# The first chunk's attention beside the third phase of the projection; scores in front of transposes; output weights by halves

## The chip, the cores and the metric

The kernel runs on one core of a Trainium2 chip. Such a core has several engines that each work through a queue of their own in order: TensorE (PE, matrix products and transposes; its weight loads are listed as PEld), VectorE (DVE), ScalarE (ACT), GpSimd (POOL) and SyncE (SP, here a queue that issues transfers). An instruction waits for the semaphores of those that it depends on, and all that stands behind it on its engine waits with it. The metric is the device time in microseconds (us) from launch to end; several runs are given, and the profile comes from one execution that was recorded in full.

## The reference

One layer of a hybrid decoder, for one prompt of 4096 tokens and for 64 sample tokens, 4160 rows in all. Three groups of heads are fed by one projection, gated, joined to a width of 1024 and projected once more:

```python
def _layer(x, conv_buf, buf_k, buf_v, mem_k, mem_v, g_pre, g_post, w_in, conv_w, sink, w_out, prompt):
    h = _rmsnorm(x, g_pre)
    z = h @ w_in
    cb, cc, ch, cg, q, k, v, ag, mq, mg = _split_cols(z)
    ...
    out_a = jax.nn.silu(cg) * cb * conv
    ...
    o_b = _window_prompt(q, k, v, sink_g)
    ...
    out_b = jax.nn.silu(ag) * o_b
    o_c = _mem_attend(mq.reshape(n, t, MEM_HEADS, HEAD_DIM), mem_k, mem_v)
    out_c = jax.nn.silu(mg) * o_c
    y = jnp.concatenate([out_a, out_b, out_c], axis=-1) @ w_out
    return x + _rmsnorm(y, g_post), new_conv, new_k, new_v
```

Group A is a gated convolution of width 3. Group B is attention with 8 query heads and 2 key heads of 64 in a window of 128 keys, with a learned sink logit per head, worked out in blocks of 128 queries against their own and the previous 128 keys. Group C is attention with 4 heads over 256 memory tokens. All is in float32.

## The kernel before

**Projection.** `input_projection` (from L841) computes z transposed, columns on the partitions, in three phases (`PHASES`, L43). A phase takes some pairs of column blocks of 128, and goes through eight blocks of 520 rows; a block is computed from seven products of halves (`PRODUCTS`, L40, a Strassen scheme over halves of 260 rows). So the steps are (phase, block, product); the third phase has 3 pairs ("quads"), 8 x 7 = 56 steps, and in each step `product` (L340) issues 36 matmuls of 128x260 over high and low parts of operands in fp32r, and `evict` (L348) adds the result from PSUM to the block's z on DVE, or copies it on ACT. `h_load` fetches the operand of three steps later into a rotating pool (`hx`, 6 buffers) and `split` (L332) makes the high part on ACT (L335) and the low part on DVE (L336). The first phase leaves the gates in DRAM (`md`) and keys and values (`qd`, `vd`), the second makes the convolution, the third the queries; a finished block is split into high and low parts (L386, L388) and stored to `qd` from SP. A step's further tasks are spread among its quads as "jobs". In the third phase the first jobs (`third_jobs`) make the memory's keys and values, then (13 steps behind the second block's start) load keys and queries of chunk 0. In the last block of this phase the output weights are loaded and split into high and low parts (`wo_load`, `wo_split`), row block by row block, left and right half of the columns in turn.

**Attention.** Prompt rows are taken in 16 chunks of 256 (`Chunk`, L978). A chunk loads keys `kst` (L998) and queries `q` (L1009) on POOL's queue, values `vT` and the gates `mix` on SP's. `values` transposes the values (L1022). A chunk has two window pairs and two cross pairs, and a pair two units. A window unit computes scores `ws` (L1093), copies and masks them into `sm` (L1095 ACT, L1096 DVE), takes the maximum (L1098), four exponentials (L1106), and divides (reciprocal, a factor of 0.5 at L1111, product at L1112); then it transposes them (`wt`, L1116), copies them out (L1118) and masks by POOL's selects (L1123 into `wpv`, L1126 in place). A cross unit has scores `xs` (L1053), maximum (L1054), exponentials (L1057), reciprocal (L1058), POOL's scale (L1061), transposes `xt` (L1066). When both units of a pair are done, `both_values` (L969, products at L976) multiplies by the values and DVE multiplies the gate in `mix` by the result (L1041, L1080).

`Pipe` staggers the units. One `start()` does, in this order: the value products of a pair whose second unit was begun three starts ago, the transposes of the unit begun two starts ago, and the scores of a new unit.

**Output projection.** `Block` (L1298) is for 128 rows: `load` the rows of x, `split` the mix into `mh` and `ml` (L1321 ACT, L1322 DVE), then `run`: for each of two halves of 512 columns, 8 row blocks of 3 matmuls `y` (L1339) with a `start()` ahead of row blocks 2 and 6; the half is multiplied by `gpost` (L1346) and squared and summed (L1347), and at the end normalised and added to x (L1357).

**Order.** Behind the projection `open_attention` closes the projection's pools (PSUM then has 3 banks for y, 2 for scores, 2 for transposes, 1 for value products). Chunks 0 and 1 follow, 16 starts with nothing between. Then `gpost` is loaded and scaled (L1296), and chunk c (from 2 on) runs beside blocks 2c-4 and 2c-3, four starts to a block. 29 blocks carry starts; the sample's attention and the last blocks follow. Outside the first phase, whose order is that of the text, a scheduler places each engine's instructions by its own estimates and due times; the engines run their queues in that order.

## Time and profile before

| | before |
|---|---|
| three runs, us | 1622.83, 1626.41, 1627.67 (median 1626.41) |
| the profiled execution, us | 1625.52 |
| its span, first to last instruction, us | 1623.8 |
| mean granted clock of TensorE | 0.992 |
| DMA packets, bytes | 175108, 305.63 MB |
| stores of q, k parts `qd` from SP | 2 x 48 issues |

The third phase lies at about 690 to 940 us, chunks 0 and 1 alone from 940 on, blocks beside chunks from 979.6 to about 1540, the sample and the last blocks to the end.

How to read the profile: busy times are shares of one execution's span. In a table of stretches each row is a window of time; the counts in brackets are instructions. A timeline row gives the start, the length, the engine, the line, the operation with output and inputs, and in square brackets the idle time before it with the instruction that ended it. Matmuls are pipelined: a modelled length of 0.39 us for a 128x512 matmul stands beside a distance of 0.23 us between starts. A float32 product (not fp32r) appears as two records.

### The profile page before, as it was taken

How to read it: one execution, taken by the hardware profiler on the slowest of the kernel's cores; microseconds unless marked ns; L12 is line 12 of the kernel's file. 1: busy time of each engine (PE TensorE's matmuls, PEld its weight loads, DVE VectorE, ACT ScalarE, POOL GpSimd, SP SyncE). 2: the span in 40 equal slices, each digit the busy share in tenths (PEclk: the TensorE clock that was granted, in tenths of full speed). 3: DMA queues.
4: the chain of work that ended last, by engine and by line, in shares of the span. 5: the costliest groups of instructions: out<-in, count | busy, mean ns of one | idle time of the engine just before them, and what ended most of it. 6: DMA issues, size and time to landing. Idle time of an engine off the chain costs nothing.

```text
span 1623.8 us, 29613 instructions
## 1 busy us (share of the span) xinstructions
PE 1579.5 (97%) x11099; PEld 1395.2 (86%) x11099; DVE 1182.6 (73%) x2131; ACT 790.8 (49%) x2023; POOL 345.8 (21%) x590
## 2 busy tenths in 40 slices
PE   9999999999999999999999979999999999999998
PEld 9999999999999999988999955777777777777766
DVE  6778888899988777964766777667776777676733
ACT  6766665565222222443443456555555555555522
POOL 0222222210000000010000035444333443443210
PEclk9999999999999999999999989999999999999999
DMA  9978999776544334699666699766666676665152
GB/s 272 206 209 225 272 284 264 270 231 231 195 171 153 119 119 147 226 291 268 205 235 251 225 281 142 139 140 140 140 153 144 151 152 144 140 140 117 53 192 91
DMA packets 175108, 305.63 MB, mean 188 GB/s; under 512 B 31093, under 2 KB 104565, under 8 KB 174933
## 3 DMA queue, kind: packets, MB, share of 16 engines
q1 hardware_dynamic: 128069, 226.76, 44.6%
q0 software_dynamic: 46176, 75.92, 24.4%
q8 instruction: 88, 1.44, 0.4%
q10 hardware_dynamic: 720, 1.05, 0.2%
q14 instruction: 55, 0.45, 0.1%
HBM read 196.54 MB, written 108.12 MB: 188 GB/s over the span
## 4 chain that ended last, share of the span: by engine, by line
PE 65%; DVE 17%; ACT 6%; issue 5%; DMA 4%; POOL 3%; SPq 0%; ACTq 0%; POOLq 0%; DVEq 0%
PE c L345 45%; PE y L1339 10%; ACT sm L1106 4%; DVE sm L1112 2%; PE wo L976 2%; PE wt L1116 2%; DVE sm L1096 2%; PE ws L1093 2%; DVE wmx L1098 1%; PE xs L1053 1%; POOL xp L1061 1%; PE xo L976 1%; PE xt L1066 1%; DVE xr L1357 1%; DVE ml L1322 1%
## 5 line engine op out<-in xcount | busy, mean ns | idle before, releaser
L1339 PE MATMUL y<-wo,mh 128*128 128x512 f32 (+1 forms) x1072 | 351.0, 391 | 2.3 <-DVE mh L1316 1.4
L352 DVE TENSOR_TENSOR z<-c,z 128x520 f32<-128x520 f32 (+1 forms) x308 | 194.3, 645 | 88.2 <-PE c L345 87.0
L1339 PEld LDWEIGHTS y<-wo,mh 128*128 128x128 f32 x1072 | 200.3, 188 | 44.2 <-issue 4.0
L1339 PE MATMUL y<-wo,ml 128*128 128x512 f32 (+1 forms) x520 | 202.7, 390 | 1.2 <-DVE ml L1322 1.2
L1106 ACT ACTIVATE sm<-sm,wnm 128x128 f32<-128x128 f32 x256 | 99.9, 391 | 76.4 <-DVE wnm L1100 76.4
L1339 PEld LDWEIGHTS y<-wo,ml 128*128 128x128 f32 x520 | 98.2, 189 | 16.4 <-DVE ml L1322 1.6
L998 POOL DMA_DIRECT2D kst<-qd x64 | 38.9, 622 | 251.3 <-DVE sm L1112 183.7
L1123 POOL TENSOR_SCALAR_AFFINE_SELECT wpv<-wpt 128x512 f32<-128x512 f32 x62 | 39.6, 638 | 222.8 <-ACT wpt L1118 222.0
L1093 PE MATMUL ws<-kst,q 128*128 128x256 f32 x512 | 79.6, 295 | 0.6 <-ACT sm L1095 0.6
L1054 DVE TENSOR_REDUCE xmx<-xs 128x2 f32<-128x512 f32 x64 | 44.1, 690 | 42.5 <-PE xs L1053 42.4
L1057 ACT ACTIVATE xp<-xs,xnm 128x256 f32<-128x256 f32 x128 | 59.3, 468 | 31.6 <-DVE xnm L1055 25.2
L1095 ACT COPY sm<-ws 128x256 f32<-128x256 f32 x128 | 44.3, 371 | 59.7 <-PE ws L1093 56.6
L711 POOL CAST wmask<-negs 128x256 uint8<-128x256 f32 x1 | 1.3, 1259 | 321.0 <-DMA negs<-in_wmask 321.0
L1061 POOL TENSOR_SCALAR xp<-xp,xrd 128x256 f32<-128x256 f32 x128 | 61.7, 488 | 36.8 <-DVE xrd L1058 34.1
L1347 ACT ACTIVATE y<-y 128x512 f32<-128x512 f32 (+1 forms) x66 | 38.8, 588 | 62.1 <-DVE yn L1346 62.0
L1093 PEld LDWEIGHTS ws<-kst,q 128*128 128x128 f32 x512 | 66.3, 191 | 2.4 <-ACT sm L1095 1.0
L1346 DVE TENSOR_TENSOR yn<-y,gpost 128x512 f32<-128x512 f32 (+1 forms) x66 | 45.0, 682 | 30.2 <-PE y L1339 29.8
L1357 DVE SCALAR_TENSOR_TENSOR xr<-yn,yst,xr 128x1024 f32<-128x1024 f32 (+2 forms) x34 | 42.5, 1252 | 28.0 <-POOL yst L1353 28.0
L1116 PEld LDWEIGHTS wt<-ident,sm 128*128 128x128 f32 x256 | 27.7, 143 | 37.7 <-ACT xp L1057 19.4
L1066 PEld LDWEIGHTS xt<-ident,xp 128*128 128x128 f32 x256 | 29.1, 141 | 33.0 <-PE wo L976 10.5
L1116 PE MATMUL wt<-ident,sm 128*128 128x128 f32 x256 | 41.8, 287 | 15.2 <-DVE xrd L1058 8.4
L1118 ACT COPY wpt<-wt 128x512 f32<-128x512 f32 x64 | 36.9, 577 | 39.2 <-PE wt L1116 38.5
(959 smaller groups left out, 5133.3 us busy)
## 6 DMA issues: line engine op xcount, KB each, us to landing
q<-qd POOLq DMA_DIRECT2D x64, 384.0 KB, 6.1
mix<-md SPq DMA_DIRECT2D x16, 1024.0 KB
xr<-in_x_p SPq DMA_DIRECT2D x32, 512.0 KB
nat<-in_x_p SPq DMA_DIRECT2D x39, 416.0 KB
o_yp<-xr SPq DMA_DIRECT2D x31, 512.0 KB
md<-th POOLq DMA_DIRECT2D x48, 260.0 KB, 6.3
qd<-zh SPq DMA_DIRECT2D x48, 260.0 KB
qd<-z SPq DMA_DIRECT2D x48, 260.0 KB
```

The lines of the kernel that those rows point to most:

```text
L345: TE.matmul(bank[:, :HW], l, r, start=first and i == 0, stop=last and i == 3 * KH - 1)
L352: add = lambda dst, other: V.tensor_tensor(dst, c, other, op=ALU.add)
L976: TE.matmul(o[cs], v[:, cs], p, start=i == 0, stop=i == n - 1, tile_position=(0, 64 * half))
L1057: S.activation(p[:, i, :], s[:, i, :], AF.Exp, bias=nm[:, i : i + 1], scale=SCALE, accum_out=den[:, i : i + 1])
L1061: G.tensor_scalar(p[:, i, :], p[:, i, :], rd[:, i : i + 1], 0.5, op0=ALU.mult, op1=ALU.mult)
L1066: TE.transpose(t[:, i * P : (i + 1) * P], p[:, i, kt * P : (kt + 1) * P], ident)
L1093: TE.matmul(s3[:, hh, :], self.q[:, 4 + 2 * (2 * half + hh) + kvh, i * P : i * P + P], self.kst[:, 2 * kvh + part, i * P : i * P + 2 * P], ...
L1106: S.activation(sm[:, hh, :], sm[:, hh, :], AF.Exp, bias=nm[:, hh : hh + 1], scale=SCALE, accum_out=den[:, hh : hh + 1])
L1116: TE.transpose(t[:, hh * P : (hh + 1) * P], sm[:, hh, :], ident)
L1339: TE.matmul(acc, self.hl[l][:, k], wo[k][c0 // 512][:, r, c0 % 512 : c0 % 512 + c1 - c0], start=j == 0, stop=j == passes * KT - 1)
L1346: V.tensor_tensor(yn[:m, c0:c1], acc[:m], gpost[:m, c0:c1], op=ALU.mult)
L1357: V.scalar_tensor_tensor(self.xr[:m, cs], yn[:m, cs], st[:m, 3:4], self.xr[:m, cs], op0=ALU.mult, op1=ALU.add)
```

## The change

- A tile `place` (8320 bytes per partition) is kept for the whole kernel. In the first two phases it holds two of the operands, and the operand pool has 4 buffers instead of 6. Later it holds the mix of every third chunk (0, 3, 6, ...), and the other two have one buffer each.
- Chunk 0 runs in the third phase. At the place where its keys and queries were loaded, `first_chunk` closes the memory's pool, opens a work pool of 5 equal buffers, loads chunk 0 with its mix, and lays out 21 pieces, one for each of the next steps: the values, then for each of four pairs (window, cross, window, cross) left scores, right scores, left transposes, right transposes, value products. The step behind the last piece loads chunk 1. PSUM has the two banks `m` of the memory's products for all of this.
- `Pipe.start` does the scores of the new unit before the transposes of the older one; the delays of two and three starts stay.
- The factor 0.5 of the window heads goes from the reciprocal (L1111, dropped) to the copy of the transposed values, which becomes a multiplication on ACT. The cross heads keep theirs.
- The output weights are loaded left half first, all eight row blocks, then the right half; block 0's mix is split in the fifth step of the last block.
- Behind the projection there is no bare stretch of starts: chunk 1's mix, two blocks of x rows and `gpost` are loaded, and blocks begin. Blocks 0 and 1 have eight starts each (ahead of row blocks 0, 2, 4 and 6 of each half): chunk 1 beside block 0, chunk 2 beside block 1; from block 2 on four as before. Block 2's split stands in the middle of block 1.
- Pools: window buffers 3 to 2; one tile for both cross transposes of a unit instead of two; keys, values and queries of chunk 0 and of odd chunks in the phase's pool, of even chunks in one pool `bp`.

```diff
-    hxp = pa.enter_context(tc.tile_pool(name="hx", bufs=6))
+    place = ctx.enter_context(tc.tile_pool(name="place", bufs=1)).tile([P, 2, KH, HW], F32, name="place")
+    hxp = pa.enter_context(tc.tile_pool(name="hx", bufs=4))
...
-    def x_load(b, o, parts=KH):
+    def x_tile(ph, b, o):
+        kept = () if ph + b == 0 else ("B11", "B21") if (ph, b) == (0, 1) else ("B12", "B22")
+        return place[:, kept.index(o)] if o in kept else hxp.tile([P, KH, HW], F32, tag="hx", name=f"x{ph}_{b}{o}")
...
+        third["pre"] = right.enter_context(tc.tile_pool(name="pre", bufs=1, side="right"))
...
         if n == 13:
-            jobs.append(lambda: chunk_load(0))
+            jobs.append(first_chunk)
+        if n > 13 and third["chunk"]:
+            jobs.append(third["chunk"].pop(0))
+        elif n > 13 and len(chunks) == 1:
+            jobs.append(lambda: chunk_load(1))
         return jobs
+    def first_chunk():
+        mem_stack.close()
+        third["work"] = mem_stack.enter_context(tc.tile_pool(name="work", bufs=5, side="right"))
+        chunk_load(0)
+        chunk = chunks[0]
+        chunk.load_mix()
+        third["chunk"] = pieces = [lambda: chunk.values(None)]
+        for left, right_, both in chunk.pairs():
+            pieces += [lambda u=u: next(u, None) for u in (left, right_) * 2] + [both]
...
     def wo_load(j):
-        k, h = divmod(j, 2)
+        h, k = divmod(j, KT)
...
             if ph == 2 and b == last and p > 0:
-                for j in range(3 * p - 3, min(3 * p, 2 * KT)):
+                for j in ((0, 1, 2), (3, 4, 5), (6, 7, 8), (9, 10), (11, 12, 13), (14, 15))[p - 1]:
                     jobs.append(lambda j=j: wo_load(j))
                     pending.setdefault(i + 1, []).append(lambda j=j: wo_split(j))
+                if p == 4:
+                    jobs.append(blocks[0].split)
...
-        mixp = ctx.enter_context(tc.tile_pool(name="mixp", bufs=2))
+        mixp = ctx.enter_context(tc.tile_pool(name="mixp", bufs=1))
+        yp = ctx.enter_context(tc.tile_pool(name="yp", bufs=2, side="right"))
-        wp = att.enter_context(tc.tile_pool(name="wp", bufs=3))
+        wp = att.enter_context(tc.tile_pool(name="wp", bufs=2))
+        bp = att.enter_context(tc.tile_pool(name="bp", bufs=1))
...
     def psum(tag, name):
+        if ps is None:
+            return third["ps"].tile([P, 512], F32, tag="m", name=name)
         return ps.tile([P, 512], F32, tag=tag, name=name, bufs={"z": 3, "s": 2, "t": 2}.get(tag, 1))
+    def work(pool, shape, tag, name, **kw):
+        if ps is None:
+            return third["work"].tile(shape, F32, tag="u", name=name)
+        return pool.tile(shape, F32, tag=tag, name=name, **kw)
...
         def start(self):
-            for both in self.third:
-                both()
-            self.third, self.second = [], self.first
-            for u, both in self.second:
-                next(u, None)
+            values, transposes = self.due.pop(self.t, ([], []))
+            at = lambda n: self.due.setdefault(self.t + n, ([], []))
+            for fn in values:
+                fn()
+            if self.waiting:
+                unit, both = self.waiting.pop(0)
+                next(unit)
+                at(2)[1].append(unit)
                 if both is not None:
-                    self.third.append(both)
-            self.first, self.new = self.new, []
-            if self.waiting:
-                self.new = [self.waiting.pop(0)]
-                next(self.new[0][0])
+                    at(3)[0].append(both)
+            for unit in transposes:
+                next(unit, None)
+            self.t += 1
...
         def drain(self):
-            while self.waiting or self.new or self.first or self.third:
+            while self.waiting or self.due:
                 self.start()
...
+        def pool(self):
+            return third["pre"] if self.c == 0 or self.c % 2 else bp
...
-            self.mix = (yp if self.c % 3 == 2 else mixp).tile([P, KT, CT], F32, tag="mix", name=f"mix{self.c}", bufs=1 if self.c % 3 == 2 else 2)
+            if self.c % 3 == 0:
+                self.mix = place.rearrange("p a k n -> p (a k n)")[:, : KT * CT].rearrange("p (k n) -> p k n", k=KT)
+            else:
+                self.mix = (yp if self.c % 3 == 2 else mixp).tile([P, KT, CT], F32, tag="mix", name=f"mix{self.c}", bufs=1)
             DMA.dma_start(self.mix, md[:, :, self.ts].rearrange("k p n -> p k n"))
...
-                vt = vp.tile([P, P], F32, tag="v", name=f"vt{self.c}_{i}")
-                S.copy(vt, t[:, 0:P])
+                if self.c == 0:
+                    vt = third["vt"] if i else third["work"].tile([P, P], F32, tag="v", name="vt0_0", bufs=1)
+                else:
+                    vt = vp.tile([P, P], F32, tag="v", name=f"vt{self.c}_{i}")
+                S.mul(vt, t[:, 0:P], 0.5)
                 self.vts.append(vt)
...
         def pairs(self):
             w, x = [self.window_pair(i) for i in range(2)], [self.cross_pair(i) for i in range(2)]
-            return [*w, *x] if self.c == 0 else [w[0], x[0], w[1], x[1]]
+            return [w[0], x[0], w[1], x[1]]
...
-            p = xp.tile([P, nb, 256], F32, tag="p", name=f"xp{c}_{h}")
+            p = work(xp, [P, nb, 256], "p", f"xp{c}_{h}")
...
+            pt = work(xp, [P, 2, CT], "xpt", f"xpt{c}_{h}", bufs=3)
             for kt in range(2):
                 t = psum("t", f"xt{c}_{h}_{kt}")
                 for i in range(nb):
                     TE.transpose(t[:, i * P : (i + 1) * P], p[:, i, kt * P : (kt + 1) * P], ident)
-                pt = xp.tile([P, CT], F32, tag="xpt", name=f"xpt{c}_{h}_{kt}", bufs=6)
-                (S.copy if kt else V.tensor_copy)(pt, t[:, :CT])
-                pts.append(pt)
+                (S.copy if kt else V.tensor_copy)(pt[:, kt], t[:, :CT])
+                pts.append(pt[:, kt])
...
-            sm = wp.tile([P, 4, P], F32, tag="sm", name=f"sm{b}_{kvh}", bufs=2)
+            sm = work(wp, [P, 4, P], "sm", f"sm{b}_{kvh}")
...
-            V.tensor_scalar(rd, rd, 0.5, None, op0=ALU.mult)
             V.tensor_tensor(sm, sm, rd.unsqueeze(2).to_broadcast([P, 4, P]), op=ALU.mult)
             yield 1
...
-            pt = wp.tile([P, 512], F32, tag="pt", name=f"wpt{b}_{kvh}")
+            pt = work(wp, [P, 512], "pt", f"wpt{b}_{kvh}")
...
-                pv = wp.tile([P, 512], F32, tag="pv", name=f"wpv{b}_{kvh}", bufs=2)
+                pv = work(wp, [P, 512], "pv", f"wpv{b}_{kvh}")
...
-    input_projection()
-    open_attention()
-    chunks[0].load_mix()
-    for c in range(2):
-        chunks[c].values(None if c == 0 else chunks[c - 1].vts[2])
-        for pair in chunks[c].pairs():
-            pipe.add(pair)
-        for i in range(8 * c, 8 * c + 8):
-            pipe.start()
-            if i == 2:
-                chunk_load(1)
-                chunks[1].load_mix()
-            if i == 9:
-                pre_stack.close()
-                yp = ctx.enter_context(tc.tile_pool(name="yp", bufs=2, side="right"))
-                chunk_load(2)
-            if i == 13:
-                chunks[2].load_mix()
-    gpost = wa.tile([P, 2, 512], F32, tag="w", name="gpost").rearrange("p a n -> p (a n)")
-    DMA.dma_start(gpost, a["gpost"].partition_broadcast(P))
-    G.tensor_scalar(gpost, gpost, float(D) ** 0.5, None, op0=ALU.mult)
...
-        def run(self, last, start):
+        def run(self, last, start, split, starts):
...
             parts = [(0, 512), (512, 768), (768, D)] if last else [(0, 512), (512, D)]
             for p, (c0, c1) in enumerate(parts):
+                if p == 1:
+                    split()
                 acc = psum("z", f"y{b}_{p}")[:, : c1 - c0]
                 j, passes = 0, 3 if m == P else 2
                 for k in range(KT):
-                    if k in (2, 6):
+                    if k in starts:
                         start()
                     for l, r in ((0, 0), (1, 0), (0, 1)) if m == P else ((0, 0), (0, 1)):
                         TE.matmul(acc, self.hl[l][:, k], wo[k][c0 // 512][:, r, c0 % 512 : c0 % 512 + c1 - c0], start=j == 0, stop=j == passes * KT - 1)
...
     blocks = [Block(b) for b in (*range(31), 32, 31)]
+    input_projection()
+    open_attention()
+    chunks[1].load_mix()
     blocks[0].load()
-    blocks[0].split()
     blocks[1].load()
-    def run(i, start):
-        if i + 1 < len(blocks) and blocks[i + 1].b != 32:
-            blocks[i + 1].split()
+    gpost = wa.tile([P, 2, 512], F32, tag="w", name="gpost").rearrange("p a n -> p (a n)")
+    DMA.dma_start(gpost, a["gpost"].partition_broadcast(P))
+    G.tensor_scalar(gpost, gpost, float(D) ** 0.5, None, op0=ALU.mult)
+    units = [8]
+    def start():
+        c, n = divmod(units[0], 8)
+        units[0] += 1
+        if n == 0 and c < NCH:
+            chunks[c].values(chunks[c - 1].vts[2])
+            for pair in chunks[c].pairs():
+                pipe.add(pair)
+        pipe.start()
+        if n == 0:
+            chunk_load(c + 1)
+        if n == 4 and c + 1 < NCH:
+            chunks[c + 1].load_mix()
+    def run(i, start, starts=(2, 6)):
+        def split():
+            if i + 1 < len(blocks) and blocks[i + 1].b != 32:
+                blocks[i + 1].split()
+        if i != 1:
+            split()
         if i + 2 < len(blocks):
             blocks[i + 2].load()
         if blocks[i].b == 32:
             blocks[i].split()
-        blocks[i].run(i == len(blocks) - 1, start)
-    for c in range(2, NCH):
-        chunks[c].values(chunks[c - 1].vts[2])
-        for pair in chunks[c].pairs():
-            pipe.add(pair)
-        n = [0]
-        def start(c=c, n=n):
-            pipe.start()
-            n[0] += 1
-            if n[0] == 1:
-                chunk_load(c + 1)
-            if n[0] == 5 and c + 1 < NCH:
-                chunks[c + 1].load_mix()
-        for i in range(2):
-            run(2 * c - 4 + i, start)
-    run(28, pipe.start)
+        blocks[i].run(i == len(blocks) - 1, start, split if i == 1 else lambda: None, starts)
+    for i in range(29):
+        run(i, start, (0, 2, 4, 6) if i < 2 else (2, 6))
     pipe.drain()
     att.close()
```

29 lines of the change are left out of this document (13 added, 16 removed).

## The prediction

> **What bounds the kernel now.** I read the page first: busy times, the slices of PE, and the chain that ended last.
>
> ```profile
> PE 1579.5 (97%) x11099; PEld 1395.2 (86%) x11099; DVE 1182.6 (73%) x2131; ACT 790.8 (49%) x2023; POOL 345.8 (21%) x590
> PE   9999999999999999999999979999999999999998
> ...
> PE 65%; DVE 17%; ACT 6%; issue 5%; DMA 4%; POOL 3%; SPq 0%; ACTq 0%; POOLq 0%; DVEq 0%
> ```
>
> TensorE bounds nearly everywhere; one slice (the 24th, about 934 to 974 us) falls below nine tenths. The change adds and removes no matmul, so any gain must come from places where PE does not issue at its pace. The table by stretches says how large this place is (columns: length, then busy time and count on PE, PEld, DVE, ACT, POOL, granted clock, DMA share, GB/s); the first row is the third phase, the last is blocks beside chunks.
>
> ```profile
> 865.00:900.00 35.00, 35.00 (x294) 35.00 (x293) 22.41 (x31) 12.54 (x16) 0.00 (x0) 1.00 0.60 215
> 940.00:950.00 10.00, 4.49 (x32) 3.65 (x30) 8.69 (x24) 6.97 (x28) 0.40 (x1) 1.00 1.04 360
> 950.00:960.00 10.00, 7.03 (x28) 4.67 (x26) 7.47 (x25) 6.57 (x28) 6.27 (x11) 0.66 1.43 251
> 960.00:970.00 10.00, 7.87 (x26) 3.88 (x26) 4.59 (x10) 2.89 (x12) 5.24 (x10) 0.66 1.66 235
> 1100.00:1200.00 100.00, 99.03 (x549) 74.81 (x548) 70.37 (x173) 54.70 (x207) 41.52 (x69) 1.00 0.72 148
> ```
>
> In the third phase PE is full, DVE 64% busy, ACT 36%, POOL idle: room for a chunk's softmax. Right behind it 26 to 32 matmuls pass in 10 us against 84 before. The timeline of PE (start, length, instruction, idle before) shows that chunk 0 runs alone there, and that the first output product comes last:
>
> ```profile
> 940.72 0.44 PE L1022 MATMUL vtp<-ident,vT 128*128 128x128 f32 x2 [0.52 <-DVE z L352]
> 949.54 0.69 PE L1116 MATMUL wt<-ident,sm 128*128 128x128 f32 x4 [4.42 <-ACT sm L1106]
> 951.22 1.09 PE L1116 MATMUL wt<-ident,sm 128*128 128x128 f32 x4 [0.99 <-ACT sm L1095]
> 961.03 1.09 PE L1116 MATMUL wt<-ident,sm 128*128 128x128 f32 x4 [3.00 <-DVE xrd L1058]
> ```
>
> Last come the waits of PE in the steady part (1020 to 1530 us: total, times, longest) and POOL's timeline at the boundary:
>
> ```profile
> PE wt L1116 <- DVE xrd L1058: 5.3, 13, 0.6
> ```
> ```profile
> 949.60 1.24 POOL L998 DMA_DIRECT2D kst<-qd  x2 [183.75 <-DVE sm L1112]
> ...
> 989.08 2.78 POOL L1296 TENSOR_SCALAR gpost<-gpost 128x1024 f32<-128x1024 f32 x1
> ```
>
> The key load of chunk 1 is issued 9.4 us after the last projection matmul (939.92, ended 940.2): it waits for the last stores of the third phase. gpost is ready only at 991.9.
>
> **Term 1, the bare stretch.** From 940.3 to 979.6 PE runs 48 ws and 24 xs, 36 transposes, 12 wo and 16 xo. In the steady timeline their starts stand 0.12, 0.105, 0.228 and 0.128 us apart: 8.6 + 3.8 + 2.7 + 2.0 = 17.1 us. Changes between kinds add about 5% (a steady chunk: 32 ws, 16 xs, 34 transposes, 16 wo, 16 xo give 15.1 us; two blocks take 38.6 us, less 96 y at 0.23 and 0.8 of waits leaves 15.7). So 18.0 of 39.3 us are work and 21.3 are lost. The two rows at clock 0.66 hold 20 x 0.34 = 6.8 us of that loss. With the change chunk 0's 21 pieces stand at steps 22 to 42 of the phase's 56, chunk 1's keys and queries are loaded in the step behind them, and the output weights and the first mix's split are ready at the end. After the last projection matmul, PE's order is vtp, ws, then y of block 0 with chunk 1 between: nothing needs the late stores. What stays is the 0.5 to 0.7 us that vtp waits for the eviction. Term: -21.3 + 0.7 = **-20.6**. Bounds: -16 (a wait of 4.4 us, the largest seen, comes back) and -21.3.
>
> The Trainium skill ("TensorE: Matmul & The Clock Gate", Part 1, on the clock gate) says that an idle window of about 3.4 us halves TensorE's clock. In the trace the second fall came with a listed wait of only 3.0 us, so the limit is not so sharp here. By the rule one such idle in the new blocks 0 and 1 would give back some 3.4 us, an estimate from that page, and the sum would be 1604.
>
> **Term 2, blocks 0 and 1.** The part from 979.6 to 1020.0 holds 184 matmuls in 40.4 us; a steady 38.6 us holds 210 or more, so 184 would take about 33.6: 7 lost (up to 9 if the kinds are weighed, y being the long ones). After the change blocks 0 and 1 have eight starts each instead of four in two blocks: chunk 1 in block 0, chunk 2 in block 1. PE has 96 x 0.23 + 2 x 15.7 = 53.5 us of work there. But chunk 2's keys and queries still wait on POOL for the stores; gpost's scale (2.8 us) and 0.62 to 0.66 us per issue follow, so issue ends about 17 us behind the last projection matmul, and landing takes 6 to 11 us more: 23 to 28. The order puts some 78 y and most of chunk 1 (17.9 + 11 = 29 us) ahead of the first product with these keys. That covers it narrowly. The first half of block 0's yn needs gpost at about 14 us and stands on DVE in front of chunk 1's last window unit; the fourth score group of PE comes at 16. Then chunk 2's eight units stand with only 18 y (4 us) between them, and DVE needs about 19 us for a chunk (27.5 us busy per steady 38.6, less 8.1 for two blocks' yn, xr and ml): 19 on DVE against 20 on PE. That is tight, so I let this part lose as much as today: **0**. Bounds: -7 (nothing lost) and +12 (rival B).
>
> **Term 3, the steady part.** In before, a window unit's transposes stand right behind a y half and wait for a chain on DVE and ACT: yn (0.68), maximum, four exps of 0.39 us, sum, reciprocal, halving (L1111, 0.17), multiply. The wait listed is 5.3 us in 13 cases and it counts from the modelled end of a y (0.39 us) while the next could start 0.23 behind its start: 13 x 0.16 = 2.1 more, 7.4. With all small ones (5.9 us listed before wt in 12.6 chunks, 24 cases) it is 5.9 + 24 x 0.16 = 9.7. I take 9.0. In after four xs products (0.47 us) stand in front of those transposes and L1111 is gone from the chain (0.5 is folded into the copy of the values, same instruction on ACT): 0.64 us of cover against a mean stall of 0.39. So it should vanish. In return a wo product at a chunk's start needs POOL's last select; POOL now has one 0.48 us scale more in front of it, and in half of the 26 places the spare time was 0.3 us in the trace: 13 x 0.2 = 2.6. Term: **-6.4**, bounds -9.7 and 0. The 64 L1111 (0.17 each, 11 us of DVE) are worth nothing elsewhere, DVE being 70% busy there.
>
> **Term 4, the third phase.** It takes chunk 0's 15.7 us of PE, which is in no term since that work is moved. A step has 36 matmuls at 0.12, 4.3 us, and becomes 5.05 with a piece. DVE has 2.9 us per step (22.41 per 35) and gets 19/21 = 0.9 more. A step with window scores is heavier: two predicated copies, maximum, four small ones, multiply, 2.9 us, so 5.8 in a step of 5.3, and the next step with little catches up. Score and transpose banks are two in all; each is used again a step later, and its readers (ACT copy 0.37, DVE copies, exps) sit in queues at most an eviction (0.7) and a split (1.24) deep. The operands have four buffers where they had six, but a load is made three steps ahead, so four suffice. SP gets two more issues (mix and values of chunks 0 and 1), POOL eight (chunk 1's keys and queries, some 0.64 us each) and 12 scales and selects, and is at 0.00 in the phase now. I set **+2** (21 pieces at 0.1), bounds 0 and, by a wait of 0.5 us per piece as at vtp, +10.5. The other moves cost nothing on the path: output weights by halves are the same 16 loads and splits one step about earlier or later, hidden under the last block, where ACT is busy 6.30 of 10 us (930 to 940); the first mix's split adds 1.2 us of DVE there. If that cover is gone it costs 2 us once.
>
> **Sum.** -20.6 + 0 - 6.4 + 2 = -25.0. The profiled execution took 1625.5 us (span 1623.8), so 1600.5; the three runs' median is 0.9 higher, which gives 1601.4. I write 1601.
>
> **Rivals.**
> A. *The steady gain is eaten.* wo waits for POOL's select in all places and takes what wt gives up. For it: half the places had 0.3 us to spare and get 0.48 us more in front. Against: the other half had 2 us. Term 3 is 0: 1600.5 + 6.4 = 1607.
> B. *The wait moves to blocks 0 and 1.* Chunk 2's keys or gpost come later than PE needs them, PE stands 5 us more, and the clock falls as it did at 950 and 960 (6.8 us). For it: the same stores, the same queue, DVE tight. Against: 78 y stand in front. Term 2 is +12: 1612.5.
> C. *Slower: the third phase stalls.* PE runs its queue in order; with two banks every score or transpose of a piece waits for a reader that stands behind evictions and splits on DVE, and the projection's matmuls stand behind it. For it: a cross unit's chain is reduce 0.69, two exps of 0.47 and small ones, near half a step, started late. Against: each piece has a whole step, and POOL, ACT are free. All 21 pieces take one of the two banks; it decides from (25 + 2)/21 = 1.3 us for each. An eviction and a split in front of the reader are 0.7 + 1.24 = 1.94, times 21 is 41 instead of 2: 1640.
> D. *All works.* Blocks 0 and 1 lose nothing more, term 2 is -7, term 4 zero: 1591.5.
> That the change doesn't do what it says would be nearly no change; the order of instructions already shows chunk 0 in the third phase, so it is only that its gain is lost later.
>
> The skill's section "A second HAM failure mode: psum-queue depth-cycling" of the same page speaks against C's cheap form: short idles between groups that cycle through banks make the clock swing. In 979 to 1000 us single waits of up to 1.2 us left the granted clock at 1.00. By the rule, half a clock in a tenth of 100 us of pieces would cost 5 us (an estimate), and the time would be 1606.
>
> **Chances and range.** Forecast (1595 to 1604) 0.46, D 0.15, A 0.13, B 0.14, C 0.07, near no change by a mixture of B and half of C 0.05. Some 0.3%, 4.9 us, is about what a measurement of this kernel can tell from no change: 1621.5 to 1631. All of C counts as slower, 0.07, the mixtures as the same, 0.05, and the rest, 0.88, as faster. The range reaches from D's 1591 to B's 1613, which leaves out C, the mixtures and the ends beyond D and B, about 0.2.
>
> **What would show it.** Right: from the last c matmul to the first y under 3 us; the granted clock 1.00 throughout; wt waits in the steady part under 2 us; the third phase longer by 16 to 18 us with PE full. Wrong: waits of c or xs on sm, xp in the third phase (C); a wait of ws on DMA or yn some 15 to 28 us behind the last c and a clock below 1.00 there (B); wo waiting on wpt more than 3 us in all (A).

## The result, and the profile after

| | before | after |
|---|---|---|
| median of 20 runs each, us | 1628.61 | 1614.24 |
| ratio to before (95% interval) | | 0.9911 (0.9893 to 0.9929) |
| the profiled execution, us | 1625.52 | 1611.36 |
| its span, us | 1623.8 | 1609.6 |
| from the first matmul to the last projection matmul (c), us | 938.4 | 953.7 |
| from there to chunk 4's value transposes (vtp), us | 134.8 | 101.4 |
| from there to chunk 15's, eleven steps of two blocks, us | 425.5 | 430.3 |
| from there to the last matmul, us | 117.1 | 116.2 |

The kernel became 14 us faster (0.9% of 1628.61); 25 were forecast, and the time lies above the range. The last four rows are differences of starts in the timeline of PE. They are the key to this case: the projection grew by 15.3 us, the stretch behind it shrank by 33.4 us, and the steady part, where the forecast had a gain of 6.4 us, grew by 4.8 us. The sum, 15.3 - 33.4 + 4.8 - 0.9 = -14.2 us, is the difference of the two spans.

The page of after, busy times and the slices of PE: the slice below nine tenths is gone.

```profile
PE 1582.0 (98%) x11099; PEld 1401.5 (87%) x11099; DVE 1157.7 (72%) x2067; ACT 791.1 (49%) x2023; POOL 364.0 (23%) x590
...
PE   9999999999999999999999999999999999999998
```

The table of stretches of after (columns as in the prediction): a stretch of the third phase with chunk 0 in it, the boundary (now at 955.5 us), and the steady part.

```profile
830.00:865.00 35.00, 35.00 (x293) 34.34 (x292) 25.67 (x47) 17.27 (x45) 6.24 (x9) 1.00 0.54 175
950.00:960.00 10.00, 8.39 (x64) 7.90 (x64) 9.89 (x17) 5.74 (x14) 0.00 (x0) 1.00 0.81 278
960.00:970.00 10.00, 10.00 (x57) 8.23 (x56) 8.59 (x25) 7.93 (x33) 2.60 (x4) 1.00 0.88 296
970.00:980.00 10.00, 9.39 (x50) 7.60 (x50) 8.42 (x20) 6.17 (x26) 8.91 (x13) 1.00 1.22 292
1100.00:1200.00 100.00, 100.00 (x541) 75.54 (x540) 66.48 (x161) 54.76 (x202) 39.74 (x62) 1.00 0.76 148
```

In the third phase PE stays full while POOL, ACT and DVE take the chunk's work. At the boundary 50 to 64 matmuls pass in 10 us instead of 26 to 32, and the granted clock is 1.00. In the steady part PE is busy 100.00 of 100 us, which looks like an improvement on 99.03, yet it issues 541 matmuls there where it issued 549 before. A full PE that issues less is the sign of what went wrong.

PE's timeline of after at the boundary: one wait, then scores of chunk 1, then the first output product, 3.1 us behind the last c (955.25).

```profile
957.13 0.44 PE L1060 MATMUL vtp<-ident,vT 128*128 128x128 f32 x2 [1.61 <-DVE z L358]
957.35 1.18 PE L1134 MATMUL ws<-kst,q 128*128 128x256 f32 x8
958.37 0.40 PE L1357 MATMUL y<-wo,mh 128*128 128x512 f32 x1
```

PE's timeline at a chunk's start in the steady part, before and then after. The wo products of the window pair: left and right half (64 columns each) run side by side, so four records of wpv and four of wpt take 1.87 us to the next instruction.

```profile
1114.99 1.08 PE L976 MATMUL wo<-wpv,vt 128*64 128x512 f32 x4
1115.90 1.03 PE L976 MATMUL wo<-wpt,vt 128*64 128x512 f32 x4
```
```profile
1095.82 0.38 PE L1060 MATMUL vtp<-ident,vT 128*128 128x128 f32 x2
1096.13 1.08 PE L1011 MATMUL wo<-wpv,vt 128*64 128x512 f32 x4
1097.04 2.09 PE L1011 MATMUL wo<-wpt,vt 128*64 128x512 f32 x4
1099.06 1.22 PE L1134 MATMUL ws<-kst,q 128*128 128x256 f32 x8
```

After, the four wpt records take 2.09 instead of 1.03 us: the left half runs alone (its two records start at 1097.04 and 1097.47), then the right (1098.06 and 1098.54). No wait is listed, since PE is busy with the left half all the while; in 1040 to 1500 us the list of PE's waits is empty. This comes at every second group of wo products, the one behind vtp (2.92 to 2.98 us eleven times, 1.87 in the others). POOL's timeline of the same place says what the right half waits for, and DVE's why it is late. First POOL before the change, at the chunk start shown above, then POOL and DVE after:

```profile
1113.06 0.65 POOL L1123 TENSOR_SCALAR_AFFINE_SELECT wpv<-wpt 128x512 f32<-128x512 f32 x1
1114.55 0.47 POOL L1061 TENSOR_SCALAR xp<-xp,xrd 128x256 f32<-128x256 f32 x1 [0.85 <-DVE xrd L1058]
1114.99 0.63 POOL L1126 TENSOR_SCALAR_AFFINE_SELECT wpt<-wpt 128x512 f32<-128x512 f32 x1
```
```profile
1094.36 0.65 POOL L1163 TENSOR_SCALAR_AFFINE_SELECT wpv<-wpt 128x512 f32<-128x512 f32 x1
1095.49 1.92 POOL L1102 TENSOR_SCALAR xp<-xp,xrd 128x256 f32<-128x256 f32 x2 [0.48 <-DVE xrd L1099]
1097.37 0.63 POOL L1166 TENSOR_SCALAR_AFFINE_SELECT wpt<-wpt 128x512 f32<-128x512 f32 x1
```
```profile
1095.84 1.23 DVE L1338 TENSOR_TENSOR ml<-place,mh 128x1024 fp32r<-128x1024 f32 x1 [0.45 <-ACT mh L1337]
```

Before, one scale stood between the two selects of the last window unit, and the select ended 0.28 us ahead of the right half's start (0.28 to 0.34 us at nearly every chunk). Scores now stand before transposes, and both scales of a cross unit stand there. They take 1.92 us, not 2 x 0.48: the first takes 0.47 us, the second 1.46, since it falls beside the block's split on DVE. The select ends at 1098.00, and the right half starts at 1098.06. It is the same at ten of the eleven chunks (second scale 1.43 to 1.46 us); at the first of them both scales take 0.47 us and it is the select itself that falls beside the split, and takes 1.61 us.

### The profile page after: what moved, and what is told of

Its sections match the earlier page's. It is cut to its first block, busy times and chain, and to the rows that moved or that the text cites. A ratio compares the mean times of both kernels' runs of the same rounds, so it can differ in the third digit from the quotient of the medians.

```text
span 1609.6 us, 29557 instructions
## 1 busy us (share of the span) xinstructions
PE 1582.0 (98%) x11099; PEld 1401.5 (87%) x11099; DVE 1157.7 (72%) x2067; ACT 791.1 (49%) x2023; POOL 364.0 (23%) x590
## 4 chain that ended last, share of the span: by engine, by line
PE 82%; DVE 6%; DMA 5%; issue 4%; ACT 1%; POOL 1%; SPq 1%; ACTq 0%; DVEq 0%; POOLq 0%
PE c L351 42%; PE y L1357 21%; PE wo L1011 5%; PE ws L1134 4%; PE xs L1094 2%; PE xo L1011 2%; PE xt L1108 2%; PE wt L1156 2%; DMA md<-th 1%; PE mem_acc L749 1%; DVE z L358 1%; DMA skm<-in_cmk 1%; DMA xm<-in_memt 1%; DMA vd<-v 0%; DMA wor<-in_w_out 0%
## 5 line engine op out<-in xcount | busy, mean ns | idle before, releaser
L1357 PE MATMUL y<-wo,mh 128*128 128x512 f32 (+1 forms) x1072 | 357.4, 400 | 1.4 <-DVE mh L1332 1.4
L1102 POOL TENSOR_SCALAR xp<-xp,xrd 128x256 f32<-128x256 f32 x128 | 85.0, 673 | 252.4 <-DVE xrd L1099 252.4
L1137 DVE COPY_PREDICATED sm<-wmask,ws 128x256 f32<-128x256 uint8 x124 | 52.1, 437 | 7.4 <-ACT sm L1136 7.3
L1166 POOL TENSOR_SCALAR_AFFINE_SELECT wpt<-wpt 128x512 f32<-128x512 f32 x64 | 44.5, 695 | 48.6 <-ACT wpt L1158 45.7
L1044 POOL DMA_DIRECT2D q<-qd x64 | 42.8, 676 | 27.6 <-DMA qd<-z 26.2
L1011 PE MATMUL wo<-wpt,vt 128*64 128x512 f32 x128 | 48.8, 600 | 0.0
```

Source lines behind the costliest of these rows:

```text
L1011: TE.matmul(o[cs], v[:, cs], p, start=i == 0, stop=i == n - 1, tile_position=(0, 64 * half))
L1102: G.tensor_scalar(p[:, i, :], p[:, i, :], rd[:, i : i + 1], 0.5, op0=ALU.mult, op1=ALU.mult)
L1137: V.copy_predicated(sm[:, 2 * half : 2 * half + 2, :], third["wmask"], third["negs"] if first else s3[:, :, 0:P])
L1166: G.affine_select(p3, p3, pattern=[[0, 4], [1, P]], compare_op=ALU.is_ge, fill=0.0, base=0, channel_multiplier=-1)
L1357: TE.matmul(acc, self.hl[l][:, k], wo[k][c0 // 512][:, r, c0 % 512 : c0 % 512 + c1 - c0], start=j == 0, stop=j == passes * KT - 1)
```

## The experiments

A profile's span is a poor measure here. From the first matmul to the last c it is 938.1 to 945.8 us in the four runs without chunk 0 in the third phase and 952.5 to 963.5 us in the ten with it. The spread within each group arises ahead of the memory's first product (`mem_acc`, 724.3 to 735.2 us behind the first matmul), although the order on PE up to there is the same in all fourteen; in e1, for one, PE stands 5.7 us at 78 us, waiting for DVE. Its cause was not followed. From that product to the last c it is 213.2 to 213.4 us without chunk 0 and 228.3 to 228.5 us with it. So beside the ratio (to the kernel before as it ran beside each experiment, with medians of 1628.15 to 1633.28 us) each run is read by the mean distance of two blocks in the steady part, from starts of vtp ten or eleven chunks apart, and by the time from the last c to the last matmul.

| run | ratio to before (95%) | two blocks, us | wo behind vtp (median), us | last c to end, us |
|---|---|---|---|---|
| before | 1 | 38.65 | 1.87 | 677.4 |
| after | 0.9911 (0.9893 to 0.9929) | 39.12 | 2.93 | 647.9 |
| e1_transposes_first | 0.9799 (0.9775 to 0.9823) | 37.85 | 1.87 | 632.9 |
| e2_values_behind_scores | 0.9851 (0.9828 to 0.9874) | 38.01 | 1.99 | 635.3 |
| e3_order_alone | 1.0008 (0.9980 to 1.0035) | 39.13 | 2.94 | 678.9 |
| e3b_fold_alone | 0.9893 (0.9866 to 0.9920) | 37.79 | 1.87 | 664.5 |
| e4_not_side_by_side | (one time, 1600.34 us) | 37.85 | 1.88 | 637.9 |
| e5_scale_on_dve | 0.9914 (0.9885 to 0.9943) | 39.22 | parted | 650.8 |
| e6_weights_by_rows | 0.9951 (0.9925 to 0.9978) | 39.13 | 2.95 | 652.4 |
| e7_first_split_late | 0.9913 (0.9889 to 0.9938) | 39.14 | 2.95 | 649.7 |
| e8_first_and_half_back | 0.9899 (0.9872 to 0.9927) | 38.87 | 1.87 | 644.8 |
| e9_half_back | 0.9949 (0.9920 to 0.9978) | 39.23 | 2.94 | 655.7 |
| e10_before_no_selects | 0.9899 (0.9866 to 0.9933) | 37.74 | 1.87 | 663.9 |
| e11_after_no_selects | 0.9875 (0.9827 to 0.9923) | 38.04 | 1.87 | 637.0 |

"Parted" in the row of e5 means that score products stand within the group.

### e1_transposes_first: the order of scores and transposes undone

```diff
         def start(self):
             ...
             for fn in values:
                 fn()
+            for unit in transposes:
+                next(unit, None)
             if self.waiting:
                 ...
-            for unit in transposes:
-                next(unit, None)
             self.t += 1
```

> The changed kernel with one thing undone: a start of the pipe does the transposes of the older unit before the scores of the new one, as before the change. Theory (the steady part lost 0.55 us per two blocks, because at every second group of wo products POOL's last select comes late and the left half runs without the right): wo groups behind vtp are back at 1.87 us from 2.93 (12 x 1.06 = 12.7 us less), wt waits of some 5 us in all come back on PE; 1614.2 - 7 = about 1607. Rival (the steady part is as good as the prediction had it and the bare stretch gave less than shown): about 1614 + 6 = 1620.

Measured: 0.9799, which is 1596 of 1628.61 us. That is more than the theory gave: wo groups are at 1.87 us, but the wt waits did not come back (PE's only wait in 1040 to 1500 us is one of 0.4 us), so two blocks take 37.85 us, less than before the change too. The rival falls. A chunk's start on PE in this run:

```profile
1139.98 0.38 PE L1060 MATMUL vtp<-ident,vT 128*128 128x128 f32 x2
1140.29 1.08 PE L1011 MATMUL wo<-wpv,vt 128*64 128x512 f32 x4
1141.20 1.03 PE L1011 MATMUL wo<-wpt,vt 128*64 128x512 f32 x4
1142.16 0.66 PE L1108 MATMUL xt<-ident,xp 128*128 128x128 f32 x4
```

This version beats both kernels. What it left open was who had removed the wt waits, since the order is that of before.

### e2_values_behind_scores: more work between vtp and the wo products

```diff
-            for fn in values:
-                fn()
             if self.waiting:
                 ...
+            for fn in values:
+                fn()
             for unit in transposes:
```

> The changed kernel, but a start does scores, then the value products, then transposes: eight ws or four xs products (0.5 to 1.0 us) now stand between vtp and the wo products. Theory (late select on POOL): the select has landed by then, all wo groups take 1.87 us, 12 x 1.06 = 12.7 us less, about 1602. Rival (the order of scores before transposes costs PE by its changes of kind, whatever POOL does): 1614, as the changed kernel.

Measured: 0.9851, wo groups behind vtp at 1.98 to 2.02 us, two blocks 38.01 us, 1.11 less than after. The order of scores before transposes is kept here and costs next to nothing (38.01 against 37.85 in e1), so the rival falls: what costs is the late select alone, and work put in front of the products hides it.

### e3_order_alone and e3b_fold_alone: the two edits of the steady part in the kernel before

e3_order_alone has both edits, e3b_fold_alone only the second, the fold of the factor 0.5 into the copy of the values:

```diff
-            for u, both in self.second:
-                next(u, None)
-                ...
             self.first, self.new = self.new, []
             if self.waiting:
                 ...
+            for u, both in self.second:
+                next(u, None)
+                ...
```
```diff
-                S.copy(vt, t[:, 0:P])
+                S.mul(vt, t[:, 0:P], 0.5)
...
-            V.tensor_scalar(rd, rd, 0.5, None, op0=ALU.mult)
```

> The kernel before, with only the steady part's edits: scores in front of transposes, and the factor 0.5 moved from the window units' reciprocals to the copy of the values. Chunk 0 stays behind the third phase. Theory (order costs 0.55 us per two blocks): 1628.6 + 7 = about 1635, no wt waits, wo groups behind vtp at 2.9 us. Rival (the prediction's term, order gains 6): 1622.

> The kernel before with one edit: the factor 0.5 moved from the window units' reciprocals to the copy of the values, which takes one DVE instruction of 0.17 us out of the chain ahead of wt. Theory (this alone ends the wt waits, which is why the order of scores and transposes had nothing left to give): two blocks take 37.8 us instead of 38.65, 12.5 times 0.85 = 10.6 us less, ratio to before 0.9935. Rival (the chain gets 0.2 us shorter per window unit and the wait only by as much): at most 24 x 0.2 = 5 us less, ratio 0.997.

Measured: with both, 1.0008, no change that can be told, and two blocks 39.13 us, as after. The steady part lost its 6 us as the theory has it (0.48 x 12), but chunk 4's vtp came 5 us earlier (129.9 us behind the last c against 134.8), so the time stayed, between theory and rival. With the fold alone, 0.9893 and 37.79 us: one small instruction less (42 ran from 1100 to 1500 us) and the wt waits are gone. The rival of e3b, 5 us at most, falls; the theory gave the size per two blocks, and why 0.2 us can do this is seen on DVE and POOL. wt starts right behind the multiply L1112 (at 1110.97 us in before, where the multiply ends at 1110.82), though the list of waits names another instruction of DVE. First the kernel before, then e3b, the same place in a chunk:

```profile
1109.54 0.17 DVE L1111 TENSOR_SCALAR wrd<-wrd 128x4 f32<-128x4 f32 x1
1109.75 1.07 DVE L1112 TENSOR_TENSOR sm<-sm,wrd 128x512 f32<-128x512 f32 x1
```
```profile
1109.64 0.63 POOL L1123 TENSOR_SCALAR_AFFINE_SELECT wpv<-wpt 128x512 f32<-128x512 f32 x1 [3.53 <-ACT wpt L1118]
1110.35 0.97 POOL L1126 TENSOR_SCALAR_AFFINE_SELECT wpt<-wpt 128x512 f32<-128x512 f32 x1
```
```profile
1109.88 0.69 DVE L1111 TENSOR_TENSOR sm<-sm,wrd 128x512 f32<-128x512 f32 x1
```
```profile
1109.98 1.09 POOL L1122 TENSOR_SCALAR_AFFINE_SELECT wpv<-wpt 128x512 f32<-128x512 f32 x1 [3.67 <-ACT wpt L1117]
1111.13 0.64 POOL L1125 TENSOR_SCALAR_AFFINE_SELECT wpt<-wpt 128x512 f32<-128x512 f32 x1
```

Before, the select starts 0.11 us ahead of the multiply; the multiply takes 1.07 instead of 0.69 us. In e3b the multiply starts 0.10 us ahead of the select; the multiply takes 0.69 and the select 1.09 instead of 0.63 us. So whichever starts first runs at its own pace and the other waits for it. The lengths fit this: the later one is longer than alone by what the earlier one still had to run, less 0.13 to 0.15 us (0.53 us left and 0.38 longer in before, 0.59 and 0.46 in e3b, the same in all 23 and 24 places). From 1040 to 1500 us of before 23 of 48 multiplies take 1.07 us, all of them beside both selects, and 12 of the 13 listed wt waits (5.1 of 5.3 us) stand behind one of these; in e3b no multiply does. Taking 0.2 us out of the chain turned the race round in half of the cases, so the chain got shorter by 0.2 + 0.38 us there.

The Trainium skill ("SBUF — State Buffer", section on the two separate sides) says that VectorE, when it reads two inputs from SBUF, and GpSimd take turns on a shared pair of ports, that the first to start holds it for its whole instruction and that the other blocks. These rows agree, but for the 0.13 to 0.15 us: 0.69 to 1.07 us on one side, 0.63 to 1.09 us on the other.

### e8_first_and_half_back and e9_half_back: the fold undone, in both orders

e8 is e1 with the factor back in the reciprocals; e9 is the changed kernel with it:

```diff
-                S.mul(vt, t[:, 0:P], 0.5)
+                S.copy(vt, t[:, 0:P])
...
             V.reciprocal(rd, den)
+            V.tensor_scalar(rd, rd, 0.5, None, op0=ALU.mult)
```

> The changed kernel with transposes before scores (as in e1_transposes_first) and also the factor 0.5 back in the reciprocals, so that of the change only the move of chunk 0, the weights by halves and the pools are left. Theory (the fold is what makes the steady part faster): two blocks 38.65 us again, 10 us above e1, about 1612, ratio to before 0.986. Rival (the steady gain of e1 comes from the mix in its kept place and the other pools): as e1, ratio 0.980.

> The changed kernel with the factor 0.5 back in the window units' reciprocals (L1111 of before), scores still in front of transposes. Theory (scores in front already cover the chain to wt; the fold then gives nothing, and the parted wo products cost the same): two blocks 39.1 us, 1614, ratio to before 0.991. Rival (the fold is worth its 10 us whatever the order): 1624, ratio 0.997.

Measured, e8: 0.9899 and 38.87 us, wt waits of 8.2 us in 23 cases are back from 1040 to 1500 us, and 11 of 47 multiplies take 1.07 us. The theory holds for the steady part, the pools do not explain e1; the 0.22 us above the 38.65 of before stay open. Only 11 of these waits (5.2 us) stand behind a multiply of 1.07 us; the other 12 (3.0 us) stand behind multiplies of 0.69 us with no select beside them, so there the fold works by its own 0.2 us. e9: two blocks 39.23 us, as the theory said: with scores in front the fold gives the steady part next to nothing (39.23 against 39.12). The four kernels with chunk 0 moved make a square: with the fold the order costs 1.27 us per two blocks (39.12 against 37.85), without it 0.36 (39.23 against 38.87), because there it also removes the wt waits. But the ratio, 0.9949, is nearer to the rival's. What is slower lies outside the steady part (104.6 us from the last c to chunk 4's vtp against 101.4, and 119.6 behind the last vtp against 116.2); that last stretch lies between 114.4 and 120.5 us over all these runs, none of which edits the sample's part, so it is not settled what of this belongs to the fold.

### e10_before_no_selects and e11_after_no_selects: the selects taken away

```diff
             if not first:
-                ...
-                G.affine_select(...)
-                steps.append((self.vts[i], pv))
-            G.affine_select(...)
+                steps.append((self.vts[i], pt))
             steps.append((self.vts[i + 1], pt))
```

> The kernel before without POOL's two selects per window unit: the products take the copied weights unmasked, so the masking by position of the window attention is left out; every matmul stays. Theory (half of the multiplies L1112 take 1.07 us instead of 0.69 because they run beside these selects, and that is most of the wt wait): all multiplies 0.69 us though L1111 is still there, wt waits of 5.9 us in the steady part fall under 2, two blocks take 37.9 to 38.2 us instead of 38.65. Rival (the wait is L1111's own 0.2 us in the chain, the selects are beside the point): 38.6 us again.

> The changed kernel without POOL's two selects per window unit, so the masking by position of the window attention is left out; every matmul stays. Theory (the wo products behind vtp take 2.93 us because the right half waits for the last select, which stands behind two cross scales): 1.87 us at every chunk, two blocks 38.05 us or a little less instead of 39.11, 12 x 1.06 = 12.7 us less in all, ratio to before about 0.983. Rival (the parting is PE's own order): 2.93 us as before.

Measured, e10: all multiplies 0.69 us though L1111 is there, no wt wait listed, two blocks 37.74 us, as with the fold. The group of multiplies from 1100 to 1500 us (busy, mean ns of one, idle before), before and in e10:

```profile
L1112 DVE TENSOR_TENSOR sm<-sm,wrd 128x512 f32<-128x512 f32 x42 | 37.1, 883 | 1.4
```
```profile
L1112 DVE TENSOR_TENSOR sm<-sm,wrd 128x512 f32<-128x512 f32 x42 | 29.1, 692 | 1.4
```

e11: wo groups 1.87 us at every chunk, two blocks 38.04 us, 1.08 less than after. Both rivals fall: the selects are the cause on both sides, by lengthening the multiply before the change and by standing behind the scales after it (the waits of e8 without a select show that the multiply's delay is not the only thing that can make wt wait). Scales still take 1.4 us or more in 23 of 96 cases in e11; they harm nobody there, because no select stands behind them.

### e5_scale_on_dve and e4_not_side_by_side: two readings of the parted products

```diff
-                G.tensor_scalar(p[:, i, :], p[:, i, :], rd[:, i : i + 1], 0.5, op0=ALU.mult, op1=ALU.mult)
+                V.tensor_scalar(p[:, i, :], p[:, i, :], rd[:, i : i + 1], 0.5, op0=ALU.mult, op1=ALU.mult)
```

> The changed kernel with the cross units' scale (128 of 0.48 us) moved from POOL to DVE. Theory (two of these scales stand in front of the last select at each chunk's start): wo groups all at 1.87 us, 12.7 us less on PE; DVE gets 128 x about 0.4 = 51 us more where it is 66% busy, hidden: about 1602 to 1605. Rival (changes of kind on PE): 1614 or more, since DVE's chain to xt does not get shorter.

Measured: 0.9914, no gain. The scales are off POOL, but the right half's last product now stands behind six score products (the scheduler places instructions by its own estimates), so that it starts 1.9 us behind the left half's instead of beside it:

```profile
1099.33 1.08 PE L1011 MATMUL wo<-wpv,vt 128*64 128x512 f32 x4
1100.24 1.02 PE L1011 MATMUL wo<-wpt,vt 128*64 128x512 f32 x2
1101.19 0.51 PE L1134 MATMUL ws<-kst,q 128*128 128x256 f32 x2
```

The run does not tell its theories apart; e11 does.

```diff
-        for i in range(n):
-            for half, steps in enumerate((left, right)):
+        for half, steps in enumerate((left, right)):
+            for i in range(n):
```

> e1_transposes_first with the value products in the order left, left, right, right instead of left, right, left, right, so that left and right halves (64 columns each) never stand next to each other at one step. Theory (halves run side by side only where they follow each other and both are ready; alone a product takes its full 0.43 to 0.52 us a pass): wo groups about 3.8 us instead of 1.87, xo about 2.0 instead of 1.03, 5.8 us more per chunk, 14 chunks beside blocks: 1602 + 75 = about 1680. Rival (the 1.06 us was waiting for the select and nothing else): groups stay at 1.87, 1602.

Measured: 1600.34 us once, wo groups 1.88 us, xo groups 1.0 us. The theory falls as far as the order of the text goes. But in the trace the two wpv products of a group still start 14 ns apart, and the two wpt products behind them, so the run does not show whether the queue held left, left, right, right and the halves ran side by side all the same, or whether the scheduler had put them in turn again. That the 1.06 us of the changed kernel is the lateness of the right half's last product, hidden in the list of waits by the left half's record, rests on e2 and e11.

### e6_weights_by_rows and e7_first_split_late: the boundary

```diff
-        h, k = divmod(j, KT)
+        k, h = divmod(j, 2)
```
```diff
-                if p == 4:
-                    jobs.append(blocks[0].split)
...
     blocks[0].load()
+    blocks[0].split()
```

> The changed kernel with the output weights loaded and split by row blocks, left and right half in turn, as before the change. If the order of halves matters, block 0's first half waits for the splits of rows 6 and 7 behind the last projection step: up to 3 us more, 1617. As the prediction has it (costs and gives nothing on the path): 1614.

> The changed kernel with block 0's mix split behind the projection instead of in its last block. The prediction's price if the cover is gone: 2 us once, 1616, seen as a wait of y on ml of about 1 to 2 us behind the first ws. Rival (ws of chunk 1 covers it): 1614.

Measured, e6: 0.9951, up to 6 us slower than after, with intervals that touch. The trace shows 1.9 us of it behind the last c (103.3 against 101.4 us to chunk 4's vtp) and 2.5 us in the last stretch, which varies by itself. No y waits for a split there; ws waits 1.8 us for xp (1.4 in after), and the granted clock is 0.85 from 990 to 1000 us, which can be 10 x 0.15 = 1.5 us. So the run does not show that the order of the weights matters, nor that it does not. e7: 0.9913, not told from after, while the trace shows y waiting 2.3 us for ml and 0.7 us for mh, a granted clock of 0.84 from 960 to 970 us, and 2.2 us more to chunk 4's vtp: the price of 2 us is right, the ratio's interval is wider than it.

## Why the prediction was right or wrong

- **Terms 1, 2 and 4, the bare stretch, blocks 0 and 1, the third phase: right in sum.** They were -20.6 + 0 + 2 = -18.6 us. Measured: 15.3 us more up to the last c and 33.4 less from there to chunk 4's vtp, -18.1 us together. That the sum is so close is partly luck: the third phase grew by 15.1 to 15.3 us where 15.7 of work and 2 of waits were set, and the stretch behind it came out at 101.4 us where 134.8 - 15.7 - 20.6 = 98.5 were due. The third phase took the chunk without new waits; at the boundary vtp waits 1.6 us instead of 0.7, and the first y comes 3.1 us behind the last c instead of under 3. The granted clock was 1.00 there with no wait above 1.6 us. e8, which keeps this part and neither edit of the steady part, confirms it: 0.9899, and 644.8 us against 677.4 behind the last c, less the 15.3 that were moved, is -17.3.
- **Rivals B and C: not seen, and of D only the third phase without waits.** Chunk 2's keys were not waited for (the waits behind the boundary are 1.4 us of ws on xp and 0.6 on sm), and the projection's matmuls did not stall.
- **Term 3, the steady part: wrong, and it is the whole miss.** The forecast was -6.4, measured +4.8 over eleven chunks. The gain, put down as 9.0 us, was near its size: the wt waits did go, and e3b has 11 x 0.86 = 9.5 us for it. The step that failed is the price, "one 0.48 us scale more in front of it" and "13 x 0.2 = 2.6". One scale more does stand there, two instead of one, and the spare 0.3 us was read rightly. But that scale falls beside a split on DVE and takes 1.43 to 1.46 us (at one chunk of the eleven the select does), so the right half is 1.06 us late at every chunk: 11 x 1.06 = 11.7 us instead of 2.6. Rival A had the right place, but by the same 0.48 us it stopped at nothing gained. -9.5 + 11.7 is +2.2; of the rest, 11 x 0.16 = 1.8 us may be the order's own cost (e2 against e1), the remainder is open.
- **What removed the wt waits was put down wrongly too.** The prediction had one cover of 0.64 us, 0.47 from the order ("after four xs products (0.47 us) stand in front of those transposes") and 0.17 from L1111. The fold alone does it, 0.86 us per two blocks in the kernel before (e3b) and 1.02 in e1 against e8, because it also wins the race that cost the multiply 0.38 us. With it the order has nothing left to give and costs 39.12 - 37.85 = 1.27 us per two blocks (e1), 39.13 - 37.79 = 1.34 in the kernel before (e3 and e3b). Fold and order together: eleven times (39.12 - 38.65) = 5.2 us, close to the 4.8 read from the timeline. What the rows had shown beforehand was a multiply of 0.69 us in some places and 1.07 in others, whose cause was not asked for. Both errors are one: two rows at their length alone, where DVE and POOL hold each other up.
- **Of the signs named for rival A, "wo waiting on wpt more than 3 us in all" would have missed it:** the list of waits shows none, because the engine is busy beside the product that waits.

## What to carry to other kernels

Ask why a row has two durations before summing its mean: here 0.69 and 1.07 us was a race between two engines, and taking 0.2 us of work out of the chain in front of it did what a reordering had been meant to do, without the reordering's price. When an order on one engine is changed, write down the new order on the queues that are fed by it, and price what then stands in front of the last instruction that a product needs, at its duration beside its neighbours and not alone. And when an engine shows 100% busy, count its instructions per 100 us.

## What was not expected of the hardware

- A DVE instruction on two tiles in SBUF and a POOL instruction hold each other up, first come first served: 0.69 against 1.07 us for the multiply, 0.63 against 1.09 us for the select, 0.48 against 1.4 us for a scale that falls beside a 1.23 us split. In each of the three pairs the later one is longer by what the earlier one still had to run, less 0.13 to 0.15 us (0.53 and 0.38, 0.59 and 0.46, 1.10 and 0.97 us). In the steady part of after POOL's scales average 716 ns, before 472 ns:

```profile
L1102 POOL TENSOR_SCALAR xp<-xp,xrd 128x256 f32<-128x256 f32 x88 | 62.3, 716 | 188.0 <-DVE xrd L1099 188.0
```
```profile
L1061 POOL TENSOR_SCALAR xp<-xp,xrd 128x256 f32<-128x256 f32 x88 | 41.1, 472 | 18.8 <-DVE xrd L1058 18.8
```

- Two products on different halves of the columns run side by side (eight records in 1.87 us), and one that waits for data leaves no idle time in the profile as long as the other half is busy (the four wpt records take 2.09 instead of 1.03 us, with no wait listed).
- The granted clock fell in 10 us of few matmuls with waits of PE of 0.7 and 2.3 us (e7, 32 matmuls, 0.84) and with one of 1.8 us (e6, 31 matmuls, 0.85), and stayed at 1.00 with one of 1.6 us among 64 matmuls (after).
